# A two-layer attention and retention encoder on one core: turned pages by way of DRAM, and a fifth pair of contraction tiles with 7 products

## The chip, the cores and the metric

The kernel runs on one core of one Trainium2 chip. The metric is the device time of one execution in microseconds (us); for the kernel before the median of three runs is taken. A profile of one execution stands beside the times. Its engines are TensorE (PE; its weight loads are PEld), VectorE (DVE), ScalarE (ACT), GpSimd (POOL), and the issuing queue SyncE (SP). DMAs are issued by SP and by POOL.

## The reference

The input is one sequence of 256 tokens of width 4096, and there are two layers. All is float32.

```python
for l in range(DEPTH):                                    # 2
    h = rmsnorm(x, norm_w[l])
    proj = h @ w_in[l]                                    # (256, 4096) @ (4096, 11264)
    aq, ak, av, ag, rq, rk, rv, rg = jnp.split(proj, SPLIT_POINTS, axis=-1)
    aq = apply_axial_rope(rmsnorm(aq, q_norm[l]), rope) * attn_scale     # 16 heads of 128
    ak = apply_axial_rope(rmsnorm(ak, k_norm[l]), rope)                  # 4 key/value heads
    a_out = silu(ag) * gqa_attention(aq, ak, av)
    r = bidirectional_retention(rope(rq), rope(rk) * ret_scale, rv, log_gf, log_gb)  # 8 heads
    r_out = silu(rg) * rmsnorm(r, ret_norm[l])
    x = x + jnp.concatenate([a_out, r_out], axis=-1) @ w_out[l]          # (4096, 4096)
return rmsnorm(x, final_norm)
```

Nearly all of the arithmetic is in the two projections with `w_in` and `w_out`. Their weights are read from DRAM once.

## The kernel before

**Projections.** The output columns are taken in blocks of two times 512: 11 blocks for `w_in` and 4 for `w_out` in each layer, 30 in all. The contraction of 4096 is cut into 32 tiles of 128, taken as 16 pairs. A block of a pair is thus a product of 2x2 blocks (two halves of 128 tokens, two tiles of the contraction, two halves of 512 columns), which plainly takes 8 products of 128x128 by 128x512. Pairs in the list `SEVEN` (0, 4, 8 and 12) take 7 products in Strassen's manner, with sums of weight blocks and of operand blocks; the other twelve take 8. The products are summed over all pairs in seven PSUM banks, `M1` to `M7`, and `combine` joins the banks on DVE into two pages of results, `ca` and `cb`.

Float32 products are made of three matmuls of rounded parts (`product`, lines 734 to 736): high by high, high by low, low by high. So each weight page of 128x1024 needs its high part `whi` (a cast on ACT) and its low part `wlo` (a subtraction on DVE). Five such pages are held in a ring. One page in each group of four pairs is "far": its low part `flo` starts as the negated high part (ACT), and a DMA from DRAM with accumulation, issued on POOL's queue (line 444), adds the weights to it. There is one far buffer, and a far page is begun when the one before has been used. The order of a block's pages is that of `pages_of`: a group starts with a pair of `SEVEN`, whose pages A, T, B and U (T and U are sums of weights, `wsum`) alternate with the pages A and B of the group's other pairs; the products of a page of `SEVEN` are 2, 2, 1 and 2, those of another page are 4.

**Operands.** The tokens' side comes as chunks of 512 features: `full`, a page of 128 features by 4 x 256 tokens. `split_pair` makes of each half a pair's parts (`x8h`, `x8l`, `x3` for 8 products, `x7h`, `x7l` for 7). Between two projections (`Turn`) the chunks 0 to 5 are stored in `next_dram` by `put` (line 577) and fetched again by `Turn.fetch` (line 600); chunks 6 and 7 are handed over in SBUF (`late`).

**Attention and retention.** They run as generators ("tasks", "lanes") that are stepped between the matmuls of later blocks: four attention groups, each with its gate and query block (`attention_group`, two `attention_pair`s in it), and four retention pairs. Where features and tokens must change places, `transposed` does it in two steps: DVE transposes a page in blocks of 32x32, and 16 copies on ACT put the blocks in their places.

```python
def transposed(src, room, dst, rest=None):
    ve.transpose(room.rearrange(flat), src.rearrange(flat))
    yield rest
    for i in range(4):
        for j in range(4):
            a, b = slice(BLK * i, BLK * (i + 1)), slice(BLK * j, BLK * (j + 1))
            ac.copy(to[b, :, :, i, :], fr[a, :, :, j, :])
        yield
```

In a layer this is done for the keys, the queries and gates of four groups, eight pages of softmax rows (`pr`), retention's keys and queries (twice each) and results (four times), and behind the first layer for the eight pages of the new x: 58 times in all. Retention's keys and queries are stored as high and low parts (`rk_dram`, `rq_dram`) and fetched for each pair of heads.

**Order of work.** There is no scheduler behind the program: the instructions stand on each engine's queue in the order in which this code emits them. A planner keeps estimated clocks of DVE and ACT (`ve`, `ac`, `now`; costs by `vector_cost`, `scalar_cost`), and between two products (`tick`) it lets a task take a step when `Weights.room` finds that the next weight pages would still be in time (`STEP_V`, `STEP_S`, `MARGIN`). Transfers are given fixed times in it (`LANDING`, `FAR_LANDING`). Nine pages of 128x1024 (`PAGES`) are shared by all tasks; `held` counts them. The profile gives most ACT and DVE instructions the line 189, that of the recording helper, so they are told apart by their tiles.

Of the kernel before, what the change touches and what calls it, by code (L numbers as in the profile page):

```python
# [41 lines left out]
STEP_V, STEP_S = 1.3, 1.7  # L42
# [4 lines left out]
LANDING = 9.0  # L47
FAR_LANDING = 14.0
MARGIN = 0.4

EARLY = 0.7

SPLITS = 3

SEVEN = (0, 4, 8, 12)
# [85 lines left out]
def is_far(group, p, k):  # L141

    return (p, k) == (group[2], PAGE_B)
# [60 lines left out]
def hybrid_encoder(  # L204
# [24 lines left out]
    next_dram = tc.dram_tile([NCH, P, KG * SEQ], F32, name="next_dram")  # L229
    x2_dram = tc.dram_tile([N_OUT, P, MT * NB], F32, name="x2_dram")  # L230
    kv_dram = tc.dram_tile([4, P, 4, SEQ], F32R, name="kv_dram")
    rk_dram = tc.dram_tile([4, P, 2, 2, SEQ], F32R, name="rk_dram")
    rq_dram = tc.dram_tile([4, P, 2, 2, SEQ], F32R, name="rq_dram")
# [8 lines left out]
    held = [0]  # L242

    def drop(n=1):

        held[0] -= n

    def page(shape, name, dt=F32):

        held[0] += 1  # L250
        return sp.tile(shape, dt, tag="pg", name=name, bufs=PAGES)
# [7 lines left out]
    junk = t(cp, [P, NB], "junk", dt=mybir.dt.bfloat16)  # L259
# [4 lines left out]
    def load_small():  # L264
        nc.sync.dma_start(dec, decay.partition_broadcast(P))

# [207 lines left out]
    late, waiting, stored, sums_of = [], [], set(), []  # L474

    def split_pair(p, v, l=None):
# [3 lines left out]
        def high(to, src):  # L480
            if not gains:
                ac.copy(to, src)
            for i, g in enumerate(gains):
                ac.activation(to[:, i, :], src[:, i, :], AF.Copy, scale=g)

        def low(to, src, hi):
            if not gains:
                ve.tensor_sub(to, src, f32(hi))
            for i, g in enumerate(gains):
                ve.scalar_tensor_tensor(  # L490
                    to[:, i, :], src[:, i, :], g, f32(hi)[:, i, :], op0=ALU.mult, op1=ALU.subtract
                )

        if p in SEVEN and gains:
            for i, g in enumerate(gains):
                ac.activation(v[:, i, :], v[:, i, :], AF.Copy, scale=g)
            yield
        x0, x1 = v[:, :, :P], v[:, :, P:]
        if p in SEVEN:
            while sums_of:  # L500
                yield
            sums_of.append(p)
            hi = t(ap, [P, 7, P], "x7h", len(SEVEN), F32R)
            lo = t(ap, [P, 7, P], "x7l", len(SEVEN), F32R)
            f = t(ap, [P, 5, P], "xf", 1)
            s1, s2, s3, s4, a22n = (f[:, i - S4, :] for i in (S1, S2, S3, S4, A22N))
            ac.activation(a22n, x1[:, 1, :], AF.Copy, scale=-1.0)
            ac.copy(hi[:, 0:2, :], x0)
            yield
            ve.tensor_sub(s1, a22n, x1[:, 0, :])  # L510
            ve.scalar_tensor_tensor(s2, s1, -1.0, x0[:, 0, :], op0=ALU.mult, op1=ALU.subtract)
            ve.tensor_sub(s3, x0[:, 0, :], x1[:, 0, :])
            ve.tensor_sub(s4, x0[:, 1, :], s2)
            yield
            ac.copy(hi[:, 2:7, :], f)
            ve.tensor_sub(lo[:, 0:2, :], x0, f32(hi)[:, 0:2, :])
            yield
            ve.tensor_sub(lo[:, 2:7, :], f, f32(hi)[:, 2:7, :])
            sums_of.pop()
        else:  # L520
# [3 lines left out]
            high(hi, v)  # L524
            yield
            low(lo, v, hi)
            ve.tensor_sub(x0, x0, x1)
            yield
            high(g[:, 0], x0)
            yield  # L530
            low(g[:, 1], x0, g[:, 0])
# [7 lines left out]
    def split_operand(c, l=None, rest=0.0):  # L539
        v, full[c] = full[c], None  # L540
        for k in range(2):
            p = 2 * c + k
            waiting.append(Lane(split_pair(p, v[:, 2 * k : 2 * k + 2, :], l)))
            waiting[-1].pair, waiting[-1].ready = p, now.t + rest
# [14 lines left out]
    def need(p, phase):  # L559

        while version[p] < phase:
            if coming(p, phase):
                split_step()
            elif turning and turning[0].step(True):
                pass
            elif late:
                split_late()
            else:
                advance()

    def put(c, v, l=None):

        full[c] = v
        if c >= NCH - 2:
            late.append((c, l))
        else:
            nc.gpsimd.dma_start(next_dram[c], v.rearrange("p k s -> p (k s)"))
            full[c] = None
            stored.add(c)
            drop()  # L580

    class Turn:
# [10 lines left out]
        def fetch(self, c):  # L593
# [4 lines left out]
            stored.remove(c)  # L598
            full[c] = page([P, KG, SEQ], "full")
            nc.gpsimd.dma_start(full[c].rearrange("p k s -> p (k s)"), next_dram[c])  # L600

        def step(self, forced=False):
            c = self.fetched
            if c < self.last and c < self.cut + 2 and (self.first or c in stored) and (held[0] < PAGES - 2 or not tasks):
# [8 lines left out]
            if self.cut == self.last:  # L613
                if self.first:
                    tasks.append(Lane(first_sums()))
# [23 lines left out]
    class Lane:  # L639
        def __init__(self, steps, heavy=True):  # L640
            self.heavy, self.tail = heavy, False
            self.steps, self.ready, self.last, self.done, self.value = steps, 0.0, 0.0, False, None

        def step(self):

            v, a = ve.until, ac.until
            rest = None
            try:
                rest = next(self.steps)
            except StopIteration as end:  # L650
                self.done, self.value = True, end.value
            if ve.until > v:
# [5 lines left out]
            if rest == "PE":  # L658
                self.ready = self.last + 2 * PASS
# [3 lines left out]
    def spawn(steps):  # L663
        lanes.append(Lane(steps))
# [5 lines left out]

    def running():

        return tasks[: 2 if len(tasks) > 1 and tasks[0].tail and not tasks[1].heavy else 1]

    def advance():

        clear()
        one = min(lanes + running(), key=lambda v: v.ready)
# [27 lines left out]
    def transposed(src, room, dst, rest=None):  # L706
# [4 lines left out]
        flat = "p m c -> p (m c)"  # L711
        ve.transpose(room.rearrange(flat), src.rearrange(flat))
        yield rest
        to = dst.rearrange("p i (m q b) -> p m i q b", m=MT, b=BLK)
        fr = room.rearrange("p m (i q b) -> p m i q b", i=4, b=BLK)
        for i in range(4):
            for j in range(4):
                a, b = slice(BLK * i, BLK * (i + 1)), slice(BLK * j, BLK * (j + 1))
                ac.copy(to[b, :, :, i, :], fr[a, :, :, j, :])
            if i == 3:  # L720
                drop()
            yield

# [8 lines left out]
    def product(out, a, b, start, stop):  # L732
# [4 lines left out]
        now.t += 3 * MM[out.shape[-1]]  # L737
# [21 lines left out]
    def rotary(v, L, kind):  # L759
# [5 lines left out]
        if kind in ("aq", "ak"):  # L765
            rs = t(sp, [P, 8], "rs", 2)
# [29 lines left out]
        oT = o.rearrange("p m (a s) -> p (m a) s", a=2)  # L796
        yield from transposed(o, v, oT)
        dst = parts_of(kind, [P, 4, SEQ])
        yield from split(dst, oT)
        drop()  # L800
        yield
        return (dst, rs) if kind == "aq" else dst
# [19 lines left out]
    def attention_pair(h, kv, qT, sgT, rs, rows_done):  # L822

        kT, v = (kv[:, 0, :], kv[:, 1, :]), [kv[:, i, :].rearrange("p (k d) -> p k d", k=MT) for i in (2, 3)]
        st = t(sp, [P, 2, 4], "st", 2)
        pr = page([P, MT, 2 * SEQ], "pr")
        for e in range(2):
            s = (yield from take_bank()).rearrange("p (m k) -> p m k", m=MT)
            for m in range(MT):
                product(s[:, m, :], at(qT, ALL, h + e, slice(m * P, (m + 1) * P)), kT, True, True)  # L830
            yield
# [16 lines left out]
            yield  # L848
        ve.reciprocal(st[:, 1, :], st[:, 1, :])
# [5 lines left out]
        rows_done.append(h)  # L855
        room = page([P, MT, NB], "room")
        prT = pr.rearrange("p m (a s) -> p (m a) s", a=2)
        yield from transposed(pr, room, prT)
        pT = parts_of("pT", [P, 4, SEQ])
        yield from split(pT, prT)  # L860
        drop()
        o = (yield from take_bank()).rearrange("p (e q) -> p e q", e=2)
        for e in range(2):
            for k in range(MT):
                product(o[:, e, :], at(v, ALL, k), at(pT, ALL, 2 * e + k), k == 0, k == MT - 1)
        yield
        drop(2)
        ve.tensor_mul(sgT[:, h : h + 2, :], o, sgT[:, h : h + 2, :])
# [3 lines left out]
    def attention_group(L, g, gacc, qacc):  # L872
        def gates():
            yield from gate(gacc, L)
            yield from transposed(gacc, page([P, MT, NB], "room"), sgT)

        kv = page([P, 4, SEQ], "kv", F32R)
        nc.gpsimd.dma_start(kv, kv_dram[g])
        sgT = gacc.rearrange("p m (a s) -> p (m a) s", a=2)
        one = spawn(gates())  # L880
        qT, rs = yield from rotary(qacc, L, "aq")
        while not one.done:
            yield
        done = []
        one = spawn(attention_pair(0, kv, qT, sgT, rs, done))
        while not done:
            yield
        yield from attention_pair(2, kv, qT, sgT, rs, done)
        while not one.done:
            yield  # L890
        drop(3)
        put(g, sgT)

    def retention_weights(L, i):

        kT = page([P, 2, 2, SEQ], "rk", F32R)
        qT = page([P, 2, 2, SEQ], "rq", F32R)
        nc.gpsimd.dma_start(kT, rk_dram[i])
        nc.gpsimd.dma_start(qT, rq_dram[i])
        dist = page([P, 2 * SEQ], "dist")  # L900
        nc.sync.dma_start(dist, consts[:, C_D:C_END])
        yield LANDING
        landed = max(now.t, L.stored) + LANDING
        D = page([P, 4, SEQ], "D")
        for e in range(2):
# [4 lines left out]
            ve.tensor_scalar_mul(v, dist, lf)  # L910
            ve.scalar_tensor_tensor(v, dist, lb, v, op0=ALU.mult, op1=ALU.min)
            yield
        drop()
        ac.activation(D, D, AF.Exp)
        yield max(landed - now.t, 0.1)
        for e in range(2):
            s = (yield from take_bank()).rearrange("p (k q) -> p k q", k=MT)
            for k in range(MT):
                product(
                    s[:, k, :],  # L920
                    (kT[:, 0, e, k * P : (k + 1) * P], kT[:, 1, e, k * P : (k + 1) * P]),
                    (qT[:, 0, e, :], qT[:, 1, e, :]),
                    True,
                    True,
                )
# [9 lines left out]
        L.weights[i] = wT  # L935
        yield
# [31 lines left out]
    def retention_pair(L, i, gacc, vacc):  # L968
        gain = page([P, NB], "gain")
        nc.sync.dma_start(gain, ret_norm[L.index, i * NB : (i + 1) * NB].partition_broadcast(P))  # L970
        v = yield from values(vacc, L)
# [414 lines left out]
```

## Time and profile before

| | |
|---|---|
| time, median of three runs | 2699.8 us (2697.59 to 2701.71) |
| the profiled execution: time, span | 2701.46 us, 2699.7 us |
| mean granted TensorE clock | 0.992 |
| PE, DVE, ACT, POOL busy | 2633.3, 2068.9, 2025.1, 218.1 us |
| matmuls | 11832 |
| moved by DMA | 644.82 MB, mean 239 GB/s |

In a row of groups the columns are the line, engine, operation, tile names (out<-in), shape and count, then the busy time in us and the mean ns of one, then the idle time of the engine just before them and what ended most of it. In a row of waits they are: who waited <- for whom, us in total, times, the longest. A row of the busy time by stage gives the stretch and its length, then the busy time of PE, PEld, DVE, ACT and POOL with the count of instructions, then the granted clock of PE, the share of the DMA engines and GB/s. A DMA queue's row gives packets, MB and the time of its packets as a share of sixteen engines over the span.

### The profile page before, as it was taken

What the parts mean: (1) busy time and instruction counts of PE and PEld (TensorE: products, weight loads), DVE (VectorE), ACT (ScalarE), POOL (GpSimd) and SP (SyncE); (2) the same over time, 40 slices, a digit from 0 to 9 for tenths busy, and PEclk for the clock granted to TensorE, in tenths of its full rate; (3) what the DMA queues carried; (4) which work ended last, traced back from release to release, by engine and by line L of the source; (5) the groups of instructions that cost most, each with busy time, mean ns of one, the idle gap of its engine ahead of it and who ended that gap; (6) DMA issues with size and microseconds to landing.
All of it is one profiled execution on the core that took longest, in us unless ns stands there. A gap on an engine that the chain in (4) does not pass through costs nothing.

```text
span 2699.7 us, 34139 instructions
## 1 busy us (share of the span) xinstructions
PE 2633.3 (98%) x11832; PEld 2182.0 (81%) x11832; DVE 2068.9 (77%) x2489; ACT 2025.1 (75%) x3176; POOL 218.1 (8%) x278
## 2 busy tenths in 40 slices
PE   6999999999999999999999999999999999999997
PEld 5878788788888888888788878887888888888886
DVE  8777787678787797766888767787778778986766
ACT  6768898887776778766987788888867777775554
POOL 0010000000100110001011100000000101000000
PEclk9999999999999999999999999999999999999998
DMA  7876677667877887888788867776678779778885
GB/s 250 279 234 218 210 223 230 202 211 231 271 247 221 286 261 223 262 257 265 266 255 246 252 191 231 212 221 209 216 244 256 238 236 306 239 221 250 248 254 183
DMA packets 191149, 644.82 MB, mean 239 GB/s; under 512 B 20736, under 2 KB 27904, under 8 KB 190976
## 3 DMA queue, kind: packets, MB, share of 16 engines
q1 hardware_dynamic: 150208, 525.19, 56.4%
q0 software_dynamic: 40768, 117.46, 19.9%
q8 instruction: 92, 1.51, 0.2%
q14 instruction: 81, 0.66, 0.1%
HBM read 612.16 MB, written 30.41 MB: 238 GB/s over the span
## 4 chain that ended last, share of the span: by engine, by line
PE 79%; DVE 7%; ACT 5%; issue 4%; DMA 4%; SPq 0%; POOL 0%; DVEq 0%; POOLq 0%; ACTq 0%
PE M L735 26%; PE M L734 25%; PE M L736 25%; DVE wlo L189 4%; DMA wraw<-in_w_in 3%; ACT pr L189 2%; ACT whi L189 2%; DMA wraw<-in_w_out 1%; PE ps L736 1%; PE ps L734 1%; PE ps L735 1%; DVE ca L189 0%; DVE cb L189 0%; DVE wsum L189 0%; ACT fhi L189 0%
## 5 line engine op out<-in xcount | busy, mean ns | idle before, releaser
L189 DVE TENSOR_TENSOR wlo<-wraw,whi 128x1024 fp32r<-128x1024 f32 x842 | 946.5, 1143 | 251.2 <-ACT whi L189 245.0
L189 ACT CAST whi<-wraw 128x1024 fp32r<-128x1024 f32 x842 | 815.2, 988 | 396.4 <-PE M L736 291.8
L735 PE MATMUL M<-wlo,x8h 128*128 128x512 f32 x1806 | 705.8, 391 | 3.3 <-DVE wlo L189 3.3
L734 PE MATMUL M<-whi,x8h 128*128 128x512 f32 x1806 | 706.1, 391 | 1.1 <-DVE ca L189 1.1
L736 PE MATMUL M<-whi,x8l 128*128 128x512 f32 x1806 | 704.8, 390 | 0.0
L735 PEld LDWEIGHTS M<-wlo,x8h 128*128 128x128 f32 x1806 | 340.8, 189 | 73.6 <-DVE wlo L189 4.1
L734 PEld LDWEIGHTS M<-whi,x8h 128*128 128x128 f32 x1806 | 340.7, 189 | 72.5 <-DVE ca L189 2.4
L736 PEld LDWEIGHTS M<-whi,x8l 128*128 128x128 f32 x1806 | 340.5, 189 | 71.5
L189 DVE TENSOR_TENSOR wlo<-wsum,whi 128x1024 fp32r<-128x1024 f32 x240 | 292.7, 1220 | 85.6 <-ACT whi L189 84.7
L189 ACT CAST whi<-wsum 128x1024 fp32r<-128x1024 f32 x240 | 252.0, 1050 | 121.2 <-PE M L736 108.3
L735 PE MATMUL M<-wlo,x7h 128*128 128x512 f32 x840 | 328.5, 391 | 10.5 <-DVE wlo L189 10.5
L736 PE MATMUL M<-whi,x7l 128*128 128x512 f32 x840 | 328.0, 390 | 6.0 <-DVE x7l L189 6.0
L734 PE MATMUL M<-whi,x7h 128*128 128x512 f32 x840 | 327.9, 390 | 0.1
L735 PE MATMUL M<-wlo,x 128*128 128x512 f32 x602 | 236.0, 392 | 12.8 <-DVE wlo L189 12.8
L734 PE MATMUL M<-whi,x 128*128 128x512 f32 x602 | 235.1, 390 | 11.6 <-ACT whi L189 11.6
L736 PE MATMUL M<-whi,x 128*128 128x512 f32 x602 | 235.0, 390 | 0.0
L189 DVE TENSOR_TENSOR wsum<-wraw 128x1024 f32<-128x1024 f32 x120 | 146.5, 1221 | 96.5 <-DMA wraw<-in_w_in 52.2
L735 PEld LDWEIGHTS M<-wlo,x7h 128*128 128x128 f32 x840 | 158.2, 188 | 44.6 <-DVE wlo L189 12.8
L736 PEld LDWEIGHTS M<-whi,x7l 128*128 128x128 f32 x840 | 158.2, 188 | 39.6 <-DVE x7l L189 6.7
L734 PEld LDWEIGHTS M<-whi,x7h 128*128 128x128 f32 x840 | 158.1, 188 | 33.5 <-DVE cb L189 0.7
L444 POOL DMA_DIRECT2D flo<-in_w_in x86 | 75.8, 881 | 1296.3 <-ACT flo L189 1086.6
L189 ACT CAST fhi<-wraw 128x1024 fp32r<-128x1024 f32 x118 | 124.2, 1052 | 73.6 <-PE M L736 64.8
(214 smaller groups left out, 3341.0 us busy)
## 6 DMA issues: line engine op xcount, KB each, us to landing
wraw<-in_w_in SPq DMA_DIRECT2D x703, 512.0 KB, 4.5
wraw<-in_w_out SPq DMA_DIRECT2D x256, 512.0 KB, 4.8
flo<-in_w_in POOLq DMA_DIRECT2D x86, 512.0 KB, 7.2
flo<-in_w_out POOLq DMA_DIRECT2D x32, 512.0 KB, 6.9
full<-next_dram POOLq DMA_DIRECT2D x18, 512.0 KB, 8.5
next_dram<-ca POOLq DMA_DIRECT2D x15, 512.0 KB, 6.1
x<-in_x SPq DMA_DIRECT2D x8, 512.0 KB, 7.1
kv<-kv_dram POOLq DMA_DIRECT2D x8, 512.0 KB, 7.8
```

What stands on the lines that cost most here:

```text
L189: return call(out, *args, **kwargs)
L444: self.adds.pop(0)[1]()
L734: nc.tensor.matmul(out, a[0], b[0], start=start, stop=False)
L735: nc.tensor.matmul(out, a[0], b[1], start=False, stop=False)
L736: nc.tensor.matmul(out, a[1], b[0], start=False, stop=stop)
```

## The change

Two things change, and the planner with them.

First, `SEVEN` becomes (0, 3, 6, 9, 12): five pairs take 7 products and eleven take 8. Groups have three pairs (the last has four), and the far page is the page B of the pairs 2, 5, 8, 11 and 14, five in a block.

Second, most pages are turned by DVE's transpose alone (`turned`), stored to DRAM with the 32x32 blocks changing places in four DMAs of 32 partitions each (`store`, pieces of 1 KB), and fetched as one page (`fetch`). The pages of keys, queries, gates and softmax rows and of retention's keys and queries get DRAM buffers of their own; results that were stored in `next_dram` anyway are stored turned. Only chunks 6 and 7 of each turn-over still have their blocks moved by 16 copies on ACT (`move`). The tokens of a turned page stand in another order inside it, so the splits read it with strided patterns (`split_turned`, `split_pair`), in more and smaller instructions where an access pattern would have too many dimensions. An attention group is cut into two tasks, `attention_group` (to the stored queries and gate) and `attention_rest`. Retention's keys and queries are stored unsplit once, and split after they have been fetched. The distances `dist` are held in SBUF, and their first scaling is done by ACT.

Third, up to three tasks run at once (`AT_ONCE`), tasks tell how many pages they will need (`need`, `own`, `pledge`), and the planner's times are other ones. The end's sums of squares are made in halves.

```diff
-STEP_V, STEP_S = 1.3, 1.7
+STEP_V, STEP_S = 1.0, 1.3
-LANDING = 9.0
-FAR_LANDING = 14.0
-MARGIN = 0.4
+LANDING = 10.0
+STORE, FETCH = 8.0, 14.0
+FAR_LANDING = 12.0
+MARGIN = 0.8
+NEED = {"ak": 4, "ag": 3, "rk": 4, "rg": 4}
+PE_REST = 1.0
+AT_ONCE = 3
-SEVEN = (0, 4, 8, 12)
+SEVEN = (0, 3, 6, 9, 12)
+FAR_PAIRS = (2, 5, 8, 11, 14)
 def is_far(group, p, k):
-    return (p, k) == (group[2], PAGE_B)
+    return k == PAGE_B and p in FAR_PAIRS
...
     def put(c, v, l=None):
-        full[c] = v
         if c >= NCH - 2:
+            full[c] = v
+            own(-1)
             late.append((c, l))
         else:
-            nc.gpsimd.dma_start(next_dram[c], v.rearrange("p k s -> p (k s)"))
-            full[c] = None
-            stored.add(c)
-            drop()
+            stored[c] = now.t + LANDING
...
+    def turned(src, room):
+        ve.transpose(
+            room.rearrange("p (b k t) -> p b k t", b=4, t=BLK),
+            src.rearrange("p m (i b e) -> p b (m i) e", i=4, e=BLK),
+        )
+    def store(room, to):
+        to = to.rearrange("(b e) (a f) -> a e b f", e=BLK, a=4)
+        for a in range(4):
+            nc.gpsimd.dma_start(to[a], room[BLK * a : BLK * (a + 1), :].rearrange("e (b f) -> e b f", b=4))
+        drop()
+    def fetch(src, name):
+        v = page([P, KG * SEQ], name)
+        nc.gpsimd.dma_start(v, src)
+        return v
...
     def rotary
-        oT = o.rearrange("p m (a s) -> p (m a) s", a=2)
-        yield from transposed(o, v, oT)
-        dst = parts_of(kind, [P, 4, SEQ])
-        yield from split(dst, oT)
+        turned(o, v)
         drop()
+        yield 0.0
+        store(v, to)
...
     def attention_pair
                 ac.activation(w, w, AF.Copy, scale=st[:, 1, 2 * e + m : 2 * e + m + 1])
-        rows_done.append(h)
-        room = page([P, MT, NB], "room")
-        prT = pr.rearrange("p m (a s) -> p (m a) s", a=2)
-        yield from transposed(pr, room, prT)
-        pT = parts_of("pT", [P, 4, SEQ])
-        yield from split(pT, prT)
+        yield
+        room = page([P, KG * SEQ], "room")
+        turned(pr, room)
+        drop()
+        yield 0.0
+        store(room, p_dram[2 * (g % 2) + h // 2])
+        yield STORE
+    def attention_values(g, h, kv, sgT):
+        pT = fetch(p_dram[2 * (g % 2) + h // 2], "pT")
+        yield FETCH
+        parts = parts_of("pT", [P, KG * SEQ])
+        yield from split(parts, pT)
...
     def attention_group
+            turned(gacc, room)
+            store(room, g_dram[g % 2])
+        rs = yield from rotary(qacc, L, "aq", q_dram[g % 2])
+        yield STORE
+    def attention_rest(L, g):
+        nc.gpsimd.dma_start(kv, kv_dram[g])
+        q = fetch(q_dram[g % 2], "q")
+        yield FETCH
...
+        sgT = fetch(g_dram[g % 2], "sgT")
+        yield from attention_values(g, 0, kv, sgT)
+        yield from attention_values(g, 2, kv, sgT)
+        nc.gpsimd.dma_start(next_dram[g], sgT)
...
     def retention_weights
-        nc.gpsimd.dma_start(kT, rk_dram[i])
-        nc.gpsimd.dma_start(qT, rq_dram[i])
-        nc.sync.dma_start(dist, consts[:, C_D:C_END])
+        raw = page([P, 2, 4 * MT, 2 * BLK], "rkq")
+        for k in range(2):
+            nc.gpsimd.dma_start(raw[:, k], src[:, :, 2 * BLK * (i % 2) : 2 * BLK * (i % 2 + 1)])
-            ve.tensor_scalar_mul(v, dist, lf)
+            ac.activation(v, dist, AF.Copy, scale=lf)
...
     def finish
-            ac.activation(junk, c[i][:, m, :], AF.Square, accum_out=sums[:, m, n : n + 1])
+            for k in range(2):
+                ac.activation(junk, c[i][:, m, k * RV : (k + 1) * RV], AF.Square, accum_out=sums[:, m, n + 2 * k : ...])
```

380 lines of the change are left out of this document (250 added, 130 removed).

## The prediction

> **What bounds the kernel now.** I read the page first, then the busy time by stage, then the waits, then the groups with shapes kept apart, then the DMA queues. The page:
>
> ```profile
> span 2699.7 us, 34139 instructions
> PE 2633.3 (98%) x11832; PEld 2182.0 (81%) x11832; DVE 2068.9 (77%) x2489; ACT 2025.1 (75%) x3176; POOL 218.1 (8%) x278
> ```
>
> TensorE (PE) is busy in 98% of the span, so two things can move the time: fewer matmuls, or fewer and shorter of the few waits of PE. VectorE (DVE) and ScalarE (ACT) average 77% and 75%, so it matters how their work lies in time. The columns of the next view are PE, weight load, DVE, ACT and POOL busy, then the granted clock, the DMA share and GB/s.
>
> ```profile
> 0.00:90.00 90.00, 69.71 (x282) 55.24 (x283) 76.00 (x130) 63.95 (x112) 2.10 (x6) 0.96 0.76 251
> 30.00:60.00 30.00, 24.01 (x98) 19.02 (x97) 28.19 (x51) 23.42 (x40) 1.02 (x1) 0.89 0.83 281
> 270.00:360.00 90.00, 87.12 (x391) 72.25 (x390) 67.37 (x73) 78.07 (x135) 6.33 (x7) 0.98 0.70 222
> 280.00:290.00 10.00, 7.67 (x30) 6.36 (x31) 9.97 (x10) 8.10 (x12) 0.00 (x0) 0.83 0.41 131
> 450.00:540.00 90.00, 87.40 (x407) 72.62 (x406) 63.95 (x71) 74.65 (x136) 4.55 (x6) 1.00 0.67 206
> 540.00:630.00 90.00, 88.34 (x407) 73.46 (x406) 68.32 (x82) 78.90 (x134) 5.20 (x5) 1.00 0.69 215
> 1530.00:1620.00 90.00, 85.55 (x385) 70.49 (x384) 66.85 (x77) 78.68 (x147) 4.25 (x4) 0.98 0.67 210
> 1800.00:1890.00 90.00, 87.38 (x394) 72.22 (x393) 64.36 (x74) 77.67 (x143) 6.31 (x7) 0.98 0.67 203
> 1890.00:1980.00 90.00, 88.36 (x412) 73.66 (x412) 64.70 (x74) 71.31 (x115) 4.03 (x5) 1.00 0.70 223
> 2250.00:2340.00 90.00, 89.52 (x412) 74.55 (x411) 82.55 (x118) 63.38 (x90) 14.48 (x21) 1.00 0.88 286
> 2430.00:2520.00 90.00, 90.00 (x399) 74.53 (x398) 61.16 (x62) 50.57 (x57) 6.95 (x8) 1.00 0.82 238
> ```
>
> The row 2430:2520 is a stage with block matmuls only: 90.00 / 399 = 0.2256 us for one, the true price of a 512-column matmul (the durations of single matmuls overlap). The six rows of the attention stages (270 to 630, 1530 to 1620, 1800 to 1980) leave PE idle 2.88 + 2.60 + 1.66 + 4.45 + 2.62 + 1.64 = 15.9 us, and there ACT is at 71 to 79 of 90 us. Three of them show a granted clock of 0.98; the row 280:290 shows how that comes about: a stall, and then a clock of 0.83 over 10 us, so 1.7 us are lost beside the stall. With three such places the attention stages lose 15.9 + 5.1 = 21 us. The waits say what it hangs on; the first two lines are of the whole span, the last two of the window 480 to 520.
>
> ```profile
> PE M L735 <- DVE wlo L189: 26.7, 15, 5.0
> DVE room L189 <- ACT pr L189: 55.4, 14, 7.1
> ...
> DVE room L189 <- ACT pr L189: 8.9, 2, 7.1
> PE M L735 <- DVE wlo L189: 2.4, 1, 2.4
> ```
>
> The 32x32 transpose of the softmax rows (room<-pr) is issued to DVE right behind their scaling on ACT. It waits there up to 7.1 us, the subtraction that makes the next wlo page is queued behind it, and PE waits for that page.
>
> **Products.** A block has 16 pairs; four with 7 and twelve with 8 products make 124, five and eleven make 123. A product is three matmuls. There are 15 blocks in each of two layers: 30 x 3 x 0.2256 = 20.3 us less of PE. Nothing hides this, since PE is the bound. Term: **-20.3**.
>
> **Vector and scalar work.** The groups with shapes kept apart:
>
> ```profile
> L189 DVE TENSOR_TENSOR wlo<-wraw,whi 128x1024 fp32r<-128x1024 f32 x722 | 870.4, 1219 | 211.5 <-ACT whi L189 205.4
> L189 ACT CAST whi<-wraw 128x1024 fp32r<-128x1024 f32 x722 | 746.9, 1050 | 341.6 <-PE M L736 237.2 <-DMA wraw<-in_w_in 40.1 <-DMA wraw<-in_w_out 31.7
> L189 DVE TENSOR_TENSOR wlo<-wsum,whi 128x1024 fp32r<-128x1024 f32 x240 | 292.7, 1220 | 85.6 <-ACT whi L189 84.7
> L189 DVE TENSOR_TENSOR wsum<-wraw 128x1024 f32<-128x1024 f32 x120 | 146.5, 1221 | 96.5 <-DMA wraw<-in_w_in 52.2 <-DMA wraw<-in_w_out 44.2
> L189 ACT ACTIVATE flo<-fhi 128x1024 fp32r<-128x1024 f32 x118 | 125.3, 1062 | 3.7
> L189 ACT COPY pr<-room 32x256 f32<-32x256 f32 x256 | 103.4, 404 | 7.6 <-DVE room L189 4.2
> L189 DVE TENSOR_TENSOR wsum<-wsum,wraw 128x512 f32<-128x512 f32 x120 | 83.0, 692 | 4.2
> L189 DVE TENSOR_TENSOR wlo<-wraw,whi 128x512 fp32r<-128x512 f32 x120 | 82.3, 686 | 39.7 <-ACT whi L189 39.6
> L189 DVE TENSOR_TENSOR wsum<-wraw,wsum 128x512 f32<-128x512 f32 x120 | 82.0, 684 | 0.0
> L189 ACT CAST whi<-wraw 128x512 fp32r<-128x512 f32 x120 | 74.2, 618 | 54.9 <-PE M L736 54.5
> ```
>
> A pair that goes from 8 to 7 products adds on DVE 1.221 + 0.692 + 0.684 (the sums) + 2 x 1.220 (their low parts) - (1.219 - 0.686) (half a page) = 4.50 us, and on ACT 2 casts at 1.050 less 0.432 = 1.67 us; over 30 blocks 135 and 50 us. The fifth far page of a block takes 1.219 us off DVE and puts a 1.062 us negation on ACT: -37 and +32 us. Of the 58 page transposes, 52 lose the 16 ACT copies of 32x256 (the other six, two chunks late at each turn-over, keep them): 52 x 16 x 0.404 = 336 us off ACT. The transposes on DVE stay. So DVE goes to about 2069 + 98 = 2167 us, 81% of the new span, and ACT to about 2025 - 254 = 1771 us, 66%. On average PE covers both. The fullest DVE stage is 2250:2340 with 82.6 of 90 us; the change adds 4.50 - 1.22 = 3.3 us to a block of 84 us, some 3.5 us to that window: 86 of 90. That still fits, with little left.
>
> **The attention stall.** The 16 ACT copies for each transpose go, 64 of them or 26 us in each attention block, and the code now gives up its turn between scaling the softmax rows and transposing them, so the transpose should no longer sit in front of a wlo page. What would be late next there is a fetch of turned data, which stands on POOL's queue and not DVE's. This term lies between 0 (a new wait takes its place) and -21; I take **-15**, as not all 21 us stand behind that one wait. The clock part of it, 5.1 us, comes behind short stalls (2.33 us idle in 280:290). The Trainium skill, "TensorE: Matmul & The Clock Gate" (Part 1), has the clock fall after an idle window of about 3.4 us; by that rule these stalls cost only themselves, the most that there is to gain is 15.9, and the sum would be some 4 us higher. The trace differs (0.83 in 280:290), and I go by it.
>
> **Transfers.** The two data queues, and the landing of the far pages' accumulating adds (the line from the answer on tile flo), and of a 128 KB load:
>
> ```profile
> q1 hardware_dynamic: 150208, 525.19, 56.4%
> q0 software_dynamic: 40768, 117.46, 19.9%
> ```
> ```profile
> DMA to landing us min/median/max: 5.2/7.1/12.0
> ```
> ```profile
> full<-in_xT SPq DMA_DIRECT2D x4, 128.0 KB, 2.6
> ```
>
> Keys, queries, gates and softmax pages (1 + 4 + 4 + 8 in a layer) now go out and come back: 34 stores and 34 fetches of 0.52 MB, 36 MB; 30 more adds make 16 MB; retention queries and keys save 8 MB, since they were stored and fetched as two parts. Net +43 MB. At the price of q1 (56.4% x 2699.7 / 525 = 2.9 us of all sixteen engines per MB) to that of q0 (4.6), this is 125 to 200 us, and the mean DMA share goes from 0.77 to 0.81 to 0.84. An attention block gets 4 stores, 4 fetches and an add, 4.7 MB or 14 to 22 us of 84: from 0.69 to 0.86 to 0.95. The trace has PE at 89.5 of 90 at a share of 0.88 (2250:2340), so I expect later landings but few stalls of PE. VectorE already waits 96 us for raw pages ahead of its sums, and there will be 150 of these instead of 120. Between 0 and +15; I take **+4**, two stalls of 2 us.
>
> POOL's queue is where a delay would count. Each store is four issues, each fetch one, and a fetch waits on that queue for its store to land, with the far adds behind it. The far pages themselves get a tighter schedule: there is one buffer, so a page is begun when the one before has been used. Between two of them lie now 27 products of 3 x 0.2256 = 0.677 us, 18.3 us; after it, in groups of three pairs, 19 products, 12.9 us (the step over a block's end keeps 27). Cast and negation take 2.1 us, the add lands 7.1 us after its issue at the median and 12.0 at most. The slack falls from 18.3 - 9.2 = 9.1 to 3.7 us at the median, and the slowest landing is 1.2 us late. If one in 20 of the 120 short steps is late by 0.7 us, that is **+4**; between 0 and +20. The Trainium skill, "DMA: Bandwidth & Descriptors" (Anatomy of one DMA), prices a POOL transfer at 2.0 us plus its bytes at 436 GB/s, an estimate of 3.2 us for an add; by it no add could be late and the term would be 0. The trace says 7.1, and that decides.
>
> **Both ends.** In the first 60 us DVE is the bound (28.19 of 30 us in 30:60 with PE at 24.01), and the first block gets 4.50 us more of it, with its second pair of 7 products earlier (pair 3, not 4): between -4 and +6, taken **+3**. At the end the squares of the last two blocks are summed in halves:
>
> ```profile
> L189 ACT ACTIVATE junk<-ps 128x256 bf16<-128x256 f32 x32 | 12.2, 383 | 9.6 <-PE ps L736 9.1
> L189 ACT ACTIVATE junk<-ca 128x512 bf16<-128x512 f32 x16 | 10.1, 629 | 10.1 <-DVE ca L189 9.9
> L189 ACT ACTIVATION_READ_ACCUMULATOR junk<-ca 128x1 f32 x32 | 6.0, 187 | 0.0
> ```
>
> Four times 0.383 + 0.187 instead of twice 0.629 + 0.187 on the chain behind the last matmul: **+0.7**.
>
> **Sum.** -20.3 - 15 + 4 + 4 + 3 + 0.7 = -23.6 us. The profiled execution took 2701.5 us (its span 2699.7), 1.7 above the median of 2699.8; from the median the sum gives **2676 us**. With every term at its good end it is -45, 2655; with the transfers, adds and start at half their bad ends and two thirds of the attention gain (-20.3 - 10 + 10 + 7 + 3 + 0.7) it is -10, 2690.
>
> **Rivals.** *Late adds (slower).* If the denser POOL traffic moves landings by 2 to 4 us, from 7.1 to 9 or 11, the 3.7 us of slack are gone for a good part: 60 of 120 short steps late by 1 us, with a half-clock stretch of 1.7 us behind one in four, cost 60 + 25 = 85 us instead of my 4, and the time is 2757. It turns slower than before once the adds cost over 28 us, about one in four late by 1 us. For it: the tight slack, and a queue with over 200 more issues. Against it: POOL is 8% busy and ACT is freed, so casts start promptly. Chance 0.10.
> *Transfers bound the attention blocks (slower).* If the stores' pieces of 1 KB cost twice 4.6 us per MB, 4 x 0.52 x 4.6 = 9.6 us more put the share of an attention block at 0.95 + 0.11 = 1.06; eight blocks of 84 us grow by 6%, 40 us, and the stall gain of 15 is gone: 2676 + 40 + 15 = 2731. For it: the 0.95 already at the upper price. Against it: at the lower price there is room to 0.86. Chance 0.08.
> *Pages run out (slower or the same).* There are nine pages, and data under way to DRAM and back keeps some of them longer; if each of the eight attention blocks stalls once for 3 us with 1.7 of slow clock, the gain in the attention stage becomes a loss of 38 in place of -15: 2729; with half of that, 2700. Chance 0.08.
> *DVE becomes the bound* in the fullest stages (86 of 90 us): some 4 us in each of four turn-overs, 2692, still faster. Chance 0.10.
> *Most stalls vanish*, also those outside attention: 2650. Chance 0.10. The forecast itself has 0.54.
>
> **How the numbers follow.** A run can tell about 0.2%, 5.4 us, from no change. Faster by more than that: forecast 0.54, DVE 0.10, vanishing stalls 0.10, less 0.03 for their upper tails: 0.71. Same: 0.08, from those tails, the half-way case of the pages and late adds at their turning point. Slower: 0.21. The range leaves out the worst of the three slow cases and the best of the good one: 2652 to 2718.
>
> **What would show it.** Right: 11070 instead of 11160 block matmuls (90 fewer), ACT under 1800 us and DVE near 2170, no wait of room for pr ahead of wlo, PE within 1 us of 90 in the attention stages, and adds that land under 10 us. Wrong: PE waiting for flo pages, PE or DVE waiting for raw pages in the attention stages with a DMA share over 0.95, or long idle stretches of POOL ended by a store's landing.

## The result and the profile after

The changed kernel takes 2659.5 us (median of 4 runs, 2656.8 to 2664.1) beside 2698.9 us for the kernel before on the same chip: a ratio of 0.9854 with a 95% interval of 0.9837 to 0.9871, or 39 us less. The forecast was 2676 us, 23.6 less, with a range of 2652 to 2718. The direction was right and the time lies in the range; the gain came out 16 us larger than the sum said. The page of the profiled execution (2660.7 us, span 2658.5):

```profile
span 2658.5 us, 33938 instructions
PE 2609.4 (98%) x11742; PEld 2164.3 (81%) x11742; DVE 2153.8 (81%) x2701; ACT 1782.2 (67%) x2518; POOL 365.0 (14%) x508
q1 hardware_dynamic: 148912, 523.35, 56.4%
q0 software_dynamic: 52896, 160.46, 26.1%
```

There are 90 matmuls fewer. DVE has gone from 2069 to 2154 us (forecast 2167) and ACT from 2025 to 1782 us (forecast 1771). The two data queues moved 41 MB more (forecast 43), and their share of the DMA engines adds up to 82.5% (forecast 81 to 84).

The busy time by stage, for the six attention stretches whose rows were shown of before, and the fullest stretches of DVE:

```profile
270.00:360.00 90.00, 90.00 (x415) 75.19 (x415) 73.99 (x85) 62.83 (x96) 19.40 (x29) 1.00 0.89 278
450.00:540.00 90.00, 89.83 (x419) 74.97 (x418) 74.60 (x89) 63.65 (x99) 18.48 (x28) 1.00 0.85 264
540.00:630.00 90.00, 87.38 (x393) 71.99 (x392) 74.53 (x91) 55.43 (x77) 12.05 (x19) 0.98 0.78 247
1530.00:1620.00 90.00, 90.00 (x416) 75.17 (x415) 73.29 (x85) 64.21 (x99) 17.92 (x27) 1.00 0.87 268
1800.00:1890.00 90.00, 89.02 (x415) 74.11 (x414) 72.87 (x88) 56.84 (x77) 16.28 (x24) 1.00 0.87 271
1890.00:1980.00 90.00, 90.00 (x415) 75.08 (x414) 77.23 (x91) 57.32 (x67) 15.77 (x23) 1.00 0.85 278
1260.00:1350.00 90.00, 87.82 (x385) 71.73 (x384) 83.80 (x143) 68.25 (x110) 14.04 (x20) 1.00 0.91 288
2250.00:2340.00 90.00, 90.00 (x410) 74.84 (x410) 83.80 (x124) 72.85 (x119) 12.28 (x14) 1.00 0.80 251
```

In the attention rows PE is idle for 0 + 0.17 + 2.62 + 0 + 0.98 + 0 = 3.8 us where it was 15.9, ACT has fallen to 55 to 64 of 90 us, and the DMA share has risen to 0.78 to 0.89. What PE waited for over the whole span (first three lines), and the landing of the far pages' adds (last line):

```profile
PE M L825 <- DVE wlo L198: 9.4, 5, 5.8
PE M L824 <- ACT whi L198: 8.9, 1, 8.9
PE M L825 <- DMA flo<-in_w_in: 5.5, 6, 2.2
```
```profile
DMA to landing us min/median/max: 5.2/7.8/12.9
```

The waits for wlo pages are down from 26.7 to 9.4 us, 5.8 of them one stall near the start. A wait that the kernel before did not have stands in the third line: six late adds, 5.5 us. The second line is the very first wait of the program.

Of the signs that the prediction named for being right, 90 matmuls fewer, ACT under 1800 us and DVE near 2170 came. PE stays within 1 us of 90 in five of the six attention rows (87.38 in 540:630), waits of `room` for `pr` are down from 55.4 to 6.2 us but not gone, and the adds land after up to 12.9 us and not all under 10. Two signs named for being wrong came as well, and cost PE little: it waits for flo pages, and POOL stands idle for stores to land, the longest time 9.5 us in front of a fetch of retention's queries.

### The profile page after: what moved, and what is told of

Read it like the earlier page. It is cut to its first block, busy times and chain, and to the rows that moved or that the text cites. A ratio compares the mean times of both kernels' runs of the same rounds, so it can differ in the third digit from the quotient of the medians.

```text
span 2658.5 us, 33938 instructions
## 1 busy us (share of the span) xinstructions
PE 2609.4 (98%) x11742; PEld 2164.3 (81%) x11742; DVE 2153.8 (81%) x2701; ACT 1782.2 (67%) x2518; POOL 365.0 (14%) x508
## 4 chain that ended last, share of the span: by engine, by line
PE 81%; DVE 8%; DMA 6%; issue 2%; ACT 2%; POOL 1%; SPq 0%; DVEq 0%; POOLq 0%; ACTq 0%
PE M L825 26%; PE M L826 26%; PE M L824 26%; DVE wlo L198 4%; DMA flo<-in_w_in 2%; DMA wraw<-in_w_in 2%; DVE wsum L198 1%; PE ps L825 1%; PE ps L824 1%; PE ps L826 1%; DMA wraw<-in_w_out 1%; ACT whi L198 1%; DMA tables<-in_k_norm 1%; DVE ca L198 0%; DVE cb L198 0%
## 5 line engine op out<-in xcount | busy, mean ns | idle before, releaser
L198 DVE TENSOR_TENSOR wlo<-wraw,whi 128x1024 fp32r<-128x1024 f32 (+1 forms) x812 | 894.9, 1120 | 281.4 <-ACT whi L198 275.4
L198 ACT CAST whi<-wraw 128x1024 fp32r<-128x1024 f32 (+1 forms) x812 | 778.8, 971 | 509.4 <-PE M L826 371.8
L824 PE MATMUL M<-whi,x8h 128*128 128x512 f32 x1536 | 600.8, 391 | 0.5 <-DVE ca L198 0.5
L825 PE MATMUL M<-wlo,x8h 128*128 128x512 f32 x1536 | 600.4, 391 | 0.0
L826 PE MATMUL M<-whi,x8l 128*128 128x512 f32 x1536 | 600.0, 391 | 0.0
L824 PE MATMUL M<-whi,x7h 128*128 128x512 f32 x1050 | 410.0, 390 | 1.5 <-DVE cb L198 1.5
L825 PE MATMUL M<-wlo,x7h 128*128 128x512 f32 x1050 | 409.4, 390 | 1.9 <-DVE wlo L198 1.9
L826 PE MATMUL M<-whi,x7l 128*128 128x512 f32 x1050 | 409.0, 389 | 0.0
L198 DVE TENSOR_TENSOR wlo<-wsum,whi 128x1024 fp32r<-128x1024 f32 x300 | 365.5, 1218 | 24.1 <-ACT whi L198 23.5
L824 PE MATMUL M<-whi,x 128*128 128x512 f32 x512 | 199.9, 390 | 11.7 <-ACT whi L198 8.9
L826 PE MATMUL M<-whi,x 128*128 128x512 f32 x512 | 200.2, 391 | 3.2 <-DVE x L198 3.2
```

Of the source, the lines that this page charges most:

```text
L198: return call(out, *args, **kwargs)
L824: nc.tensor.matmul(out, a[0], b[0], start=start, stop=False)
L825: nc.tensor.matmul(out, a[0], b[1], start=False, stop=False)
L826: nc.tensor.matmul(out, a[1], b[0], start=False, stop=stop)
```

## The experiments

Each ratio is to the kernel before on the same chip. The theory after the result: the 39 us are two separate gains of about 20 us, the fifth pair's matmuls and the end of the attention stalls, and what is left there are late adds. The rivals: one of the two does it all; it is the load of ACT and not the order on DVE's queue that made the stalls; transfers or DVE are about to become the bound.

**The parts alone.** The first run turns pages by way of DRAM, without the fifth pair:

```diff
-SEVEN = (0, 3, 6, 9, 12)
-FAR_PAIRS = (2, 5, 8, 11, 14)
+SEVEN = (0, 4, 8, 12)
+FAR_PAIRS = (2, 6, 10, 14)
```

> The changed kernel with SEVEN back at (0, 4, 8, 12) and the far pages at pairs 2, 6, 10 and 14, so only the turned pages' way through DRAM and the planner are new. Theory (two separate gains): the 90 matmuls come back, +20.3 us, and the waits for flo pages (5.5 us in the changed kernel, some 7 with the clock behind them) go, as a far page has 27 products of lead again: 2659 + 20 - 7 = 2672 us, no PE wait for flo, attention stages with PE at 90 of 90. Rival (the fifth pair pays only a little, most came from the turning): under 2665. Rival (the turning alone loses by its transfers, and the products carry all): 2690 or more.

Measured: 2678.6 us, ratio 0.9925 (0.9908 to 0.9941). PE never waits for a flo page, and all six attention rows have PE at 90.00 of 90. Its longest waits are these: splits of operands, two stalls of 4.9 us at the turn-overs; the program's first wait; a split near the start; wlo pages.

```profile
PE M L824 <- ACT x L198: 9.8, 2, 4.9
PE M L824 <- ACT whi L198: 9.1, 2, 8.9
PE M L826 <- DVE x7l L198: 5.0, 1, 5.0
PE M L825 <- DVE wlo L198: 3.4, 4, 1.4
```

So the turning with its planner gives 21 us, and the fifth pair 19 us on top, near the 20.3 us of its matmuls. The run is 6 us above the expectation. It has two stalls at the turn-overs that the changed kernel has not, 9.8 us with (by the trace's clock records) some 5.1 us of slow clock behind them, and it lacks the changed kernel's 5.8 us stall near the start and the 3.4 us of slow clock behind that: 14.9 - 9.2 = 5.7 us. Why these stalls come and go was not tested.

The second run puts the fifth pair into the kernel before. Its nine pages do not go round with it unless the fetch of a stored chunk asks for one more free page, so this was changed too, and a control has that alone.

```diff
-SEVEN = (0, 4, 8, 12)
+SEVEN = (0, 3, 6, 9, 12)
-            ... (held[0] < PAGES - 2 or not tasks):
+            ... (held[0] < PAGES - 3 or not tasks):
```

> The kernel before with SEVEN at (0, 3, 6, 9, 12), far page at the third pair of each group, everything else as before, but for the fetch of a stored chunk, which asks for one more free page (nine pages do not go round otherwise). Theory: -20.3 us for the products, the attention stalls stay at 21 us, and late adds cost 4 us: about 2683 us. Rival (VectorE cannot carry the fifth pair while ScalarE still copies blocks): stalls in the attention stages double, 2700 us or more.

> The kernel before, whose fetch of a stored chunk asks for one more free page: the control for the run of the fifth pair alone, which had this too. Theory (the fifth pair is what slowed that run by 107 us): within 5 us of 2700 us. Rival (the later fetches did it): 2750 us or more.

Measured: 2806.8 us, ratio 1.0395 (1.0379 to 1.0411), with the fifth pair; 2718.9 us, 1.0064 (1.0049 to 1.0079), for the control. The control is 17 us slower, more than expected, with new waits of PE for operand splits (12.6 us in two stalls of 6.3) at the turn-overs. On top of that the fifth pair costs 88 us, although it takes 20 us of matmuls away. PE's longest waits in that run, and a stretch of its attention stage:

```profile
PE M L735 <- DMA flo<-in_w_in: 32.2, 13, 10.1
PE M L735 <- DVE wlo L189: 22.0, 14, 4.8
PE M L734 <- ACT whi L189: 18.0, 7, 10.7
PE ps L734 <- ACT aqh L189: 15.4, 4, 4.0
PE M L735 <- DMA flo<-in_w_out: 12.9, 6, 3.8
```
```profile
450.00:540.00 90.00, 87.37 (x403) 71.92 (x403) 72.18 (x81) 84.77 (x149) 5.46 (x7) 1.00 0.69 217
```

Late adds stop PE 19 times in that run (45 us). In the stretch shown PE is idle no longer than before, but ACT is at 85 of 90 us; in 900:990, where the longest of these waits lies, PE has 79.1 of 90 us at a clock of 0.94. The adds land about as soon as before (7.5 us at the median, 7.1 before); they are begun late.

**Order on DVE's queue, or load of ACT?** One run adds to the kernel before only a step boundary between the scaling of the softmax rows and their transpose; one takes that boundary out of the changed kernel:

```diff
         rows_done.append(h)
+        yield
         room = page([P, MT, NB], "room")
```

> The kernel before with one step boundary more, between the scaling of the softmax rows on ACT and their transpose on DVE; the 16 ACT copies stay. Theory (order on DVE's queue): the transpose no longer stands in front of a wlo page, DVE waits for pr fall from 55 us to under 15, PE's waits in the attention stages go, 2680 us. Rival (load of ACT): the copies are what delays whi and with it wlo, so the stalls stay: 2695 to 2700 us.

> The changed kernel without the step boundary between the scaling of the softmax rows and their transpose. Theory (order on DVE's queue): DVE waits for pr again, 40 us or more in all, PE stalls of 2 to 3 us come back in the attention stages, 2672 to 2680 us. Rival (load of ACT): ACT without the copies is done with the scaling soon enough, 2657 to 2663 us.

Measured: 2684.0 us, ratio 0.9943 (0.9928 to 0.9958), for the boundary alone; 2673.4 us, 0.9902 (0.9887 to 0.9917), for the changed kernel without it. The transposes' rows of groups, of before, with the boundary alone, of after, and of after without it, in this order:

```profile
L189 DVE STREAM_TRANSPOSE room<-pr 128x1024 f32<-128x1024 f32 x16 | 19.9, 1244 | 55.4 <-ACT pr L189 55.4
```
```profile
L189 DVE STREAM_TRANSPOSE room<-pr 128x1024 f32<-128x1024 f32 x16 | 19.9, 1244 | 18.4 <-ACT pr L189 18.2
```
```profile
L198 DVE STREAM_TRANSPOSE room<-pr 128x1024 f32<-128x1024 f32 x16 | 19.9, 1243 | 6.6 <-ACT pr L198 6.2
```
```profile
L198 DVE STREAM_TRANSPOSE room<-pr 128x1024 f32<-128x1024 f32 x16 | 19.9, 1244 | 33.1 <-ACT pr L198 33.0
```

The transpose takes 1.24 us in each; what differs is how long DVE stands in front of it. In the six attention rows PE is idle for 15.9 us before, 4.2 with the boundary alone, 3.8 after, and 8.4 after without it. Sixteen instructions moved behind a step boundary are worth 16 us in the old kernel and 14 in the new one. The order on DVE's queue made most of these stalls; ACT's load alone did not, as its copies are all still there in the first run (ACT 2025.1 us). The waits for `pr` moved less than expected, to 18.4 us and not under 15 with the boundary, and to 33.1 and not 40 without it.

**What stopped the fifth pair in the old kernel.** The same boundary was added to the run with the fifth pair, and in another run 12 of the 16 ACT copies of each page (but for the two late chunks of the new x) were left out instead, so that blocks stay in the wrong places:

> The kernel before with the fifth pair (and the stricter fetch), and with the step boundary between the scaling of the softmax rows and their transpose. Theory (it is ACT's copies that leave no room for the fifth pair, since far pages are cast late): the boundary gives its 16 us and no more, 2785 to 2795 us. Rival (order on DVE's queue was what the fifth pair made worse): 2740 us or less.

> The kernel before with the fifth pair (and the stricter fetch), leaving out 12 of the 16 ACT copies of each transposed page but for the two late chunks of the new x, so blocks stay in the wrong places: 56 x 12 x 0.404 = 271 us off ACT, no transfer added. Theory (ACT's copies leave no room for the fifth pair): most of the 107 us go, 2680 to 2710 us, with waits of PE for flo under 15 us. Rival (the one-task-at-a-time planner and its pages, or VectorE's load, stop the fifth pair): 2760 us or more.

```diff
-                ac.copy(to[b, :, :, i, :], fr[a, :, :, j, :])
+                if every or j == 0:
+                    ac.copy(to[b, :, :, i, :], fr[a, :, :, j, :])
```

Measured: 2801.3 us, ratio 1.0375 (1.0355 to 1.0395), with the boundary: only 5 us better, less than expected. With few copies 2717.9 us, 1.0055 (1.0039 to 1.0072): 89 us better, down to the level of the control. From the starts and ends of single instructions in the traces: between the last matmul on a far page and the cast of the next, one in four had over 2.4 us with the fifth pair, over 0.1 us with few copies, and over 0.1 us in the changed kernel. That delay comes straight off a slack of 3.7 us. PE's waits for adds with few copies:

```profile
PE M L736 <- DMA flo<-in_w_in: 20.5, 7, 5.2
PE M L736 <- DMA flo<-in_w_out: 3.4, 1, 3.4
```

So it is the block copies on ACT that leave no room for the fifth pair: without most of them its loss against the control is gone. A run with few copies and four such pairs was not made, so it is open how much of the 89 us the copies cost without the fifth pair. The expected 2680 to 2710 us was missed: it left out the 17 us of the stricter fetch, and waits for flo are 24 us and not under 15. For most of these 24 us the trace shows the cause. An add is issued 0.3 us after its negation at the median, but five of the late ones, 17 us of PE's waits, 4.6 to 5.5 us after it. Four of the five stood on POOL's queue behind the fetch of retention's queries, which waits there for its store to land, and one behind the fetch of a stored chunk. A row of single instructions gives the start, the length, the engine, line, operation and tiles, and in brackets the idle time before and what ended it:

```profile
1971.69 0.53 POOL L900 DMA_DIRECT2D rq<-rq_dram  x1 [4.55 <-DMA rq_dram<-rql]
1972.48 0.88 POOL L444 DMA_DIRECT2D flo<-in_w_in  x1 [0.26 <-issue]
```

The two longest waits of the fifth pair alone, 10.1 and 8.6 of its 45 us, are of this kind too: these adds were issued 10.1 and 9.2 us after their negations, behind the same fetch. These waits come of the order on POOL's queue and not of ACT's copies directly.

**What limits the changed kernel now.** Three far pages instead of five, the low parts of the other two on DVE (`FAR_PAIRS = (2, 8, 14)`); and each store piece issued a second time into DRAM that nothing reads:

> The changed kernel with three far pages in a block (pairs 2, 8 and 14) instead of five, so that each has 27 products or more of lead; the low parts of the other two are made on VectorE, 2 x 1.22 us more for each block, 73 us in all. Theory (the short lead is what is left of the attention stalls): no wait for flo pages, some 7 us gained, 2652 us, if VectorE at 84% still covers. Rival (VectorE is at its end): waits for wlo pages grow, 2665 us or more.

> The changed kernel with each of the 208 store pieces issued a second time, into DRAM that nothing reads: 27 MB more on the POOL queue. Theory (the transfers are hidden, with room left): PE waits for raw pages stay at none, only the adds land somewhat later, 2660 to 2670 us. Rival (the transfers are close to being the bound in the attention blocks): each of the eight blocks grows by the 4 x 0.52 MB x 3 us = 6 us of its extra transfers, 2700 us or more.

With three far pages: 2720.0 us, ratio 1.0068 (1.0053 to 1.0083). Waits for flo are gone, but the gain is too, and more:

```profile
PE M L824 <- ACT x L198: 33.4, 8, 6.1
```
```profile
990.00:1080.00 90.00, 81.60 (x350) 66.11 (x349) 73.69 (x107) 55.05 (x81) 5.13 (x7) 0.92 0.62 194
```

DVE's total rises to 2228 us, 82%. The operand splits are made at the last moment: eight stalls of up to 6.1 us, one at the start and seven behind the turn-overs, with slow clocks behind them (0.92 in 990:1080). The rival was right in its sign, though not in its place: waits for wlo pages hardly grow (11.9 us, 9.4 in the changed kernel). Nor is an engine full there: in the row shown DVE is at 74 and ACT at 55 of 90 us. That the planner puts the splits off because it counts DVE as too full is a reading of the program, not tested. In the six attention rows, meanwhile, PE keeps 89.2 to 90 of 90.

With the second stores: 2696.6 us, ratio 0.9983 (0.9973 to 0.9993), 37 us more than the changed kernel.

```profile
PE M L830 <- DMA flo<-in_w_in: 20.8, 9, 5.2
PE M L830 <- DVE wlo L198: 13.5, 8, 5.4
PE M L830 <- DMA flo<-in_w_out: 5.7, 4, 3.6
```
```profile
1800.00:1890.00 90.00, 85.68 (x382) 70.42 (x382) 69.42 (x79) 58.16 (x86) 27.17 (x44) 0.98 0.89 286
```

The theory (2660 to 2670) missed, and the rival comes near the time but has not the mechanism: PE waits 26.5 us for late adds instead of 5.5, with the clock behind them (0.98 in the row shown). The prediction's rival of the late adds is what the changed kernel stands next to: 208 more issues with 27 MB on POOL's queue bring it about. It is not the landing that grows, though: 8.0 us at the median and 11.7 at most, beside 7.8 and 12.9 in the changed kernel. Eight of the 13 late adds, 20 of the 26.5 us, were issued 4.2 to 6.5 us after their negations, all behind the eight pieces of a doubled store, which take POOL some 4.4 us to issue:

```profile
506.34 0.62 POOL L786 DMA_DIRECT2D p_dram<-room  x1 [8.38 <-DVE room L198]
...
510.24 0.55 POOL L787 DMA_DIRECT2D s_dram<-room  x1
510.78 1.00 POOL L469 DMA_DIRECT2D flo<-in_w_in  x1
```

Is it the queue? The fetches of turned pages were issued on SP's queue instead, then those of stored chunks too (both with the early tables below):

> The changed kernel with the early tables, and the fetches of turned queries, keys, gates and softmax pages issued on SP's queue instead of POOL's. Theory (adds are late where they are queued on POOL behind fetches): adds land sooner, median below 7.5 us, PE's waits for flo fall from some 10 us to 3 or less, 2645 us. Rival (all sixteen engines are shared, so the queue does not matter): as with the early tables alone, 2654 us. Rival (a fetch that waits for its store now holds up the raw pages behind it on SP): waits for raw pages grow, 2665 us or more.

> As the run before it, and the fetches of stored chunks at the turn-over on SP's queue too. Theory: 1 to 3 us less than that one. Rival (raw pages held up at the turn-over): 5 us or more above it.

2654.8 us (0.9830, 0.9816 to 0.9845) and 2655.5 us (0.9832, 0.9817 to 0.9848), both like the early tables alone. The adds, first and second run:

```profile
DMA to landing us min/median/max: 5.0/7.9/11.6
```
```profile
DMA to landing us min/median/max: 5.1/7.9/11.6
```

At the median they land no sooner than with the early tables alone (7.7), and PE's waits for flo stay at 8.3 and 8.0 us, where 3 or less were expected. So in this kernel the moved fetches are not what makes adds late. The stores stayed on POOL's queue in both runs, and there the delay shows: of the four longest waits for adds in the changed kernel, three are of adds issued 1.5 to 2.8 us after their negations, behind the four pieces of a store, and the fourth is the landing of 12.9 us. A run with the stores on another queue was not made.

**A better version.** The 5.8 us stall near the start was DVE in front of its rotary tables: DVE waited 8.8 us for them. Their load was moved ahead of the values, and the task asks for one more page:

```diff
-NEED = {"ak": 4, "ag": 3, "rk": 4, "rg": 4}
+NEED = {"ak": 5, "ag": 3, "rk": 4, "rg": 4}
...
     def keys_values(L, kacc, vacc):
+        L.tables = {}
+        L.plain = plain_tables(L.index)
         v = yield from values(vacc, L)
...
-        L.tables = {}
-        L.plain = plain_tables(L.index)
         yield from rotary(kacc, L, "ak", k_dram)
```

> The changed kernel with the rotary tables of the attention keys loaded before the values are made, not after. Theory (the 5.8 us stall of PE at 156 us is VectorE standing in front of its tables, 8.8 us): stall and half clock behind it go, 8 to 9 us less, 2651 us. Rival (the task is late anyhow, and something else stalls there): 2656 to 2660 us.

2654.2 us, ratio 0.9818 (0.9801 to 0.9834), 5 us less than the changed kernel, with its interval just clear of the changed kernel's; the 2651 us expected were not reached. With the two runs above, which had the early tables too, it is the fastest. The stretch with the stall, after and with early tables:

```profile
140.00:170.00 30.00, 24.21 (x95) 19.44 (x94) 21.11 (x32) 16.58 (x32) 5.43 (x5) 0.89 0.69 200
```
```profile
140.00:170.00 30.00, 30.00 (x134) 24.82 (x134) 29.25 (x46) 20.68 (x37) 7.36 (x9) 1.00 0.90 272
```

39 matmuls more in the same 30 us are 8.8 us, as expected; part of it is given back, above all in waits for flo, 10.8 us against 5.5 in the changed kernel.

## Why the prediction was right, and where its sizes were off

- **Products, -20.3.** Right: 19 us between the turning alone and the whole change. That the two numbers lie so near is in part luck, since the stalls of these two runs differ and happen to cancel: PE is idle for 48.5 and 49.1 us in their profiles, at a clock of 0.993 in both. That the products pay at all is not a matter of course: in the old kernel the same step loses 88 us. The prediction had no term for this, as it costed the two parts as if they were independent.
- **Attention stall, -15.** The mechanism was right and the size was too small. The term reached to -21, and the row's sums give it almost in full: 15.9 us of idle PE and 5.1 of slow clock became 3.8 and 1.7, and the 3.8 are late adds. I had held back 6 us for stalls with another cause; none were left in those rows. Most of it is the boundary: alone it gives 16 us.
- **Adds, +4.** Right in kind, somewhat more in size: six waits, 5.5 us, and 1.7 us of half clock at 540:630. The slack is as worked out, the landing 7.8 us and not 7.1. The sum took every add as issued at once; three of the four longest waits have POOL's store issues in them. The rival of the late adds had landings grow by 2 to 4 us, which no run shows, not even the one with the stores doubled (8.0). Its turning point was also set too far out: with its own slow clock behind one late add in four, 28 us are reached at about one in six late by 1 us, not one in four. By the Trainium skill's price ("DMA: Bandwidth & Descriptors", Anatomy of one DMA), an estimate of 3.2 us, no add could have been late; the traces disagree.
- **Transfers, +4.** Too high: no wait of PE for raw pages. DVE's wait for raw pages ahead of its sums fell, from 96 to 45 us, although there are 150 instead of 120. The share of an attention block came out at the lower price (0.78 to 0.89).
- **Start and end, +3 and +0.7.** Near: in the first 180 us before has made 649 matmuls and after 640, 2.0 us behind, with the 5.8 us stall in it, which the term did not foresee. From the end of the last matmul to the end of the span it is 16.4 us before and 17.4 after, 1.0 longer.
- **Not in the sum.** The stretch 1260:1350, the turn-over between the layers: before it had 86.14 us of PE at a clock of 0.98, after 87.82 at 1.00, some 3.5 us better. This was no step of mine.

Together: -20 (products) - 21 (attention) + 7 (adds) + 0 (transfers) + 2 and 1 (start and end) - 3.5 (turn-over) = -35 of the 41 us between the spans; the other 6 us are spread over stretches in which no single wait stands out. The terms that were mis-sized are the attention stall (6 us too small), the transfers (4 us too large) and the turn-over (missing), with the adds 3 us the other way. Of the rivals, DVE as the bound did not show at 83.8 of 90 us; with 75 us more on it (three far pages) the kernel loses 60 us, but in splits put off while DVE is at 74 of 90. Late adds show with the stores doubled.

## What to carry to other kernels

Look at what stands in front of an instruction on an in-order engine before counting the engine's load: sixteen transposes issued one step too early cost 16 us on an engine that was 77% busy. A step that saves work on the bound can lose far more than it saves if its helpers have no room; make the room first (here ACT's block copies), then take the step, and test the parts alone. When a buffer is refilled by a transfer, work out the lead in products and set it against the slowest landing, not the median, and add what the transfer may wait on the queue of the engine that issues it.

## What was not expected of the hardware

Short waits of PE were enough to slow its clock. In 540:630 after, PE waits 2.2 us for one add, and the row behind that wait shows a clock of 0.83 over 10 us, 1.7 us lost; the trace's clock records have 3.4 us at half clock there.

```profile
550.00:560.00 10.00, 9.02 (x33) 7.25 (x33) 7.20 (x10) 3.81 (x5) 0.88 (x1) 0.83 0.60 189
```

Not every such wait does it: before, one of 2.4 us in 450:540 left the clock at 1.00. The Trainium skill, "TensorE: Matmul & The Clock Gate" (Part 1), names an idle window of about 3.4 us for this; the rows of both kernels show it after shorter waits. And 512 KB adds land after 7.0 to 8.0 us at the median in every run, whether or not the fetches of turned pages stand on the same queue.
